# Seven products of half the tokens in place of eight in the MLP's second product

## The chip, the cores and the metric

The kernel runs on one core of a Trainium2 chip. Its engines work side by side: TensorE (PE, with its weight loads PEld) multiplies matrices, VectorE (DVE), ScalarE (ACT) and GpSimd (POOL) do the elementwise work, SyncE (SP) issues most DMAs. The metric is the device time of one execution in microseconds (us). The kernel before takes 2743.2 us, the median of 3 runs from 2741.49 to 2745.22.

## The reference

The reference runs two blocks of a hybrid sequence model on 512 tokens of width 1024 in float32: two layers with gated scans and a convolved feed-forward, and then one layer with four mixers and an MLP. Only the end of that last layer is touched here:

```
hn  = rms(x, norm2_g)
hid = square(relu(hn @ w_mlp1))      # [512, 1024] @ [1024, 4096]
x   = x + hid @ w_mlp2               # [512, 4096] @ [4096, 1024]
```

## The kernel before

Activations lie with features on the 128 partitions and the 512 tokens along the free dimension, so the width of 1024 is KD = 8 tiles and the hidden width of 4096 is 32 tiles. To keep float32 accuracy at the speed of the type fp32r, every operand of a large product is split in two: a high half, rounded by ACT (`activation(..., AF.Copy)`), and a low half, the rest, taken by DVE as a subtraction. A product of a 128 x 128 block of weights with a tile of activations is then three matmuls, high x high, high x low and low x high (`mm3`, which calls `mm`, line 257). They are called split matmuls here, in contrast to the matmuls of small fp32 operands, of which the trace keeps two records each.

`gemm` makes one output tile of 128 features: `weights` loads eight blocks (128 x 1024, 512 KB) through SP into wr, ACT writes wh (line 245), DVE writes wl (line 246), and PE adds up all inner tiles in one of the two banks `pd` of PSUM.

`mlp` works in two halves of 16 hidden tiles. In each, 16 calls of `gemm` make hidden tiles (24 split matmuls each); DVE takes a tile from PSUM times the norm's factor (line 394), squares its positive part (line 1140), and the tile is split into xh (line 286, ACT) and xl (line 287, DVE). Then 8 calls of `gemm` with 48 split matmuls each make the second product of this half, and DVE adds it to the tiles mac, which hold the residual x. After the second half each mac goes to the output. POOL has no part in it.

Pools hand out buffers in turn: wr has 3, wh and wl 2 each, `pd`, `pr` and `pl` 2 banks each. The order in which the instructions stand on each engine is made by the framework's scheduler from the program; each engine then runs its own list strictly in that order, and an instruction that waits holds up all behind it. Three places of that order, before and now, are shown with the change.

Of the kernel before, what the change touches and what calls it, by code (L numbers as in the profile page):

```python
# [8 lines left out]
F32 = mybir.dt.float32  # L9
F32R = mybir.dt.float32r  # L10
U8 = mybir.dt.uint8
AF = mybir.ActivationFunctionType
ALU = mybir.AluOpType
# [4 lines left out]
P = 128  # L18
T = 512
D = 1024  # L20
KD = 8
# [3 lines left out]
LN_NQ = math.log(64.0 ** -0.5)  # L25
DFF1 = 2816
NF1 = 22


def _cols(v):  # L30
# [143 lines left out]
class Net:  # L174
# [77 lines left out]
        self.mm(ps, lo, xh, start=False, stop=stop)  # L252

    def mm(self, *a, **k):
        """a matmul; those of a paced stretch are queued behind the steps of a scan, a few after each"""
        if not self.pace:
            return self.nc.tensor.matmul(*a, **k)  # L257
        with self.tc.issue_after(self.pace[0]):
            self.nc.tensor.matmul(*a, **k)  # L259
        self.paced += 1  # L260
        if self.paced % PACE == 0:
            self.pace.pop(0)

    def gemm(self, srcs, xs, lo="v", m=P):
        bank = self.bank("pd")
        ps = bank[:m]
        nk = sum(s.shape[1] for s in srcs)
        k = 0
        for s in srcs:
            hi, lw = self.weights(s, lo)  # L270
            for i in range(s.shape[1]):
                self.mm3(ps, hi[:, i], lw[:, i], xs[k][0], xs[k][1], k == 0, k == nk - 1)
                k += 1
        return bank

    def split(self, src, gain=None, lo="v", pool=None):
        pl, th, tl = (self.xs, "xs", "xs") if pool is None else (pool[0], f"h{pool[1]}", f"l{pool[1]}")
# [47 lines left out]
        return st["xs"], rb  # L325

    def norm2_end(self, st):
        """the final norm of the first block and the first of the second in one"""
        nc = self.nc
        r, o = self.rtile(), self.rtile()  # L330
        pa, pb = self.sumsq_bc(st["a"]), self.sumsq_bc(st["b"])
        self.rsqrt(r, pa, 1.0 / D, 0)
        nc.vector.tensor_tensor(o, r, r, op=ALU.mult)
        nc.vector.tensor_tensor(o, o, pb, op=ALU.mult)
        self.rsqrt(o, o, 1.0 / D, 0)
        nc.vector.tensor_tensor(o, o, r, op=ALU.mult)
        return st["xs"], o, r
# [57 lines left out]
        return out  # L395

    def gdn_small(self, l, xs, rb, sp):
        """token-major gates of all heads: columns (c, d*4+h)"""
        nc = self.nc
        ps = self.gemm([self.I[f"w_ba{l}"]], xs, m=16)  # L400
        bt = sp.tile([16, T], F32, name=self.nmx("bt"), tag="bt")
# [74 lines left out]

    @staticmethod
    def pair(t, width, b, first, off, n):
        """columns off .. off + n of a tile [P, 2 * width], blocks of b taken in turn from its halves, from half `first` at the start"""
        return bass.AP(tensor=t.tensor, offset=t.offset + off + first * width, ap=[list(t.ap[0]), [2 * b, n // (2 * b)], [b + (1 - 2 * first) * width, 2], [1, b]])  # L480

    def gdn_inverse(self, l, h, sm, gp, front):
# [336 lines left out]
            return self.norm2_end(st) if last else self.norm_end(st)  # L819

    def gemm_tok(self, w, xs, n, rb, pool, tmp, tag):
        """a bank [tokens, 4, n]"""
        t = self.evac(self.gemm([w], xs, m=n)[:n], rb[:n], pool, *tmp, part=n)
        ps = self.bank(tag, shape=(P, 4, n))
        for c in range(4):
            self.nc.tensor.transpose(ps[:, c], t[:, c * P:(c + 1) * P], self.mk("ident")[:n, :n])
        return ps

    def fold_final(self):
        """fin * norm1 gains, used while the last FFN of the first block leaves"""  # L830
        self.fg = self.cp.tile([P, KD], F32, name="fg1")
        self.nc.vector.tensor_tensor(self.fg, self.col("fin", 0, 8), self.col("n1", 0, 8), op=ALU.mult)

# [295 lines left out]
    def mlp(self, state):  # L1129
        nc, tc = self.nc, self.tc  # L1130
        V, A = nc.vector, nc.scalar
        xs, rb = state
        M1, M2 = self.I["w2_m1"], self.I["w2_m2"]
        with tc.tile_pool(name="ml", bufs=1) as ml:
            acc = []
            for half in range(2):
                hs = []
                for m in range(16):
                    h = self.evac(self.gemm([M1[16 * half + m]], xs), rb, ml, "mh", 2)
                    V.scalar_tensor_tensor(h, h, 0.0, h, op0=ALU.max, op1=ALU.mult)  # L1140
                    hs.append(self.split(h, pool=(ml, m)))
                for m in range(KD):
                    ps = self.gemm([M2[m][:, 16 * half + a:16 * half + a + 8] for a in (0, 8)], hs)
                    if half == 0:
                        a = ml.tile([P, T], F32, name=self.nmx("mac"), tag=f"mac{m}")
                        nc.scalar.dma_start(a, self.xd[m])
                        V.tensor_tensor(a, a, ps, op=ALU.add)
                        acc.append(a)
                    else:
                        V.tensor_tensor(acc[m], acc[m], ps, op=ALU.add)  # L1150
                        nc.sync.dma_start(self.O["out"][m], acc[m])


def place_tables(nc):
    """Loads of activation tables, each for the longest run of functions that one set serves"""
    from concourse.hw_specs import get_activation_tables

    sets = {n: {str(f) for f in fs} for n, fs in get_activation_tables("trn2").items()}
# [26 lines left out]
    for i, (b, l) in enumerate(work):  # L1185
        out = []
# [33 lines left out]
```

## Time and profile before

| | |
|---|---|
| profiled execution | span 2742.3 us |
| median of the runs | 2743.2 us, 0.9 us above the span |
| busy in the span | PE 96%, DVE 57%, ACT 41%, POOL 12% |
[...]
| DMA | 254.13 MB, mean 93 GB/s |

The span runs from the first to the last instruction of the one execution that the profiler recorded. The MLP is its end, from about 2399 us on: the hidden tiles of the two halves lie up to about 2487 us and from 2564 to 2651 us, the second products behind them. Lines are numbered as in the kernel printed above. A matmul's duration in the trace reaches from its start until its result is complete; the next one starts earlier, so the time that one costs PE is the distance of two starts. DMA issues and semaphores are not counted as busy.

### The profile page before, as it was taken

How to read it: one execution, taken by the hardware profiler on the slowest of the kernel's cores; microseconds unless marked ns; L12 is line 12 of the kernel's file. 1: busy time of each engine (PE TensorE's matmuls, PEld its weight loads, DVE VectorE, ACT ScalarE, POOL GpSimd, SP SyncE). 2: the span in 40 equal slices, each digit the busy share in tenths (PEclk: the TensorE clock that was granted, in tenths of full speed). 3: DMA queues.
4: the chain of work that ended last, by engine and by line, in shares of the span. 5: the costliest groups of instructions: out<-in, count | busy, mean ns of one | idle time of the engine just before them, and what ended most of it. 6: DMA issues, size and time to landing. Idle time of an engine off the chain costs nothing.

```text
span 2742.3 us, 32455 instructions
## 1 busy us (share of the span) xinstructions
PE 2645.3 (96%) x12674; PEld 2178.6 (79%) x12674; DVE 1556.6 (57%) x2234; ACT 1124.7 (41%) x1511; POOL 329.2 (12%) x282
## 2 busy tenths in 40 slices
PE   7999899999999979998999999999999999999999
PEld 4788788878888857887888788888777788888887
DVE  6778764455554366778644555534874444553442
ACT  6545544343333255455443433333446443332221
POOL 1112320001110011122200011100100111000000
PEclk9999989999999999999999999999999999999999
DMA  4112212253223332111123423234411232433332
GB/s 149 62 49 67 62 39 68 88 167 100 94 98 114 121 89 70 55 61 54 39 76 101 160 95 100 93 121 127 145 64 51 82 96 94 140 129 99 94 104 88
DMA packets 99064, 254.13 MB, mean 93 GB/s; under 512 B 10016, under 2 KB 31520, under 8 KB 98656
## 3 DMA queue, kind: packets, MB, share of 16 engines
q1 hardware_dynamic: 66960, 215.17, 24.5%
q10 hardware_dynamic: 31568, 35.85, 4.5%
q8 instruction: 100, 1.64, 0.2%
q0 software_dynamic: 384, 1.05, 0.1%
q14 instruction: 52, 0.43, 0.1%
HBM read 238.36 MB, written 12.62 MB: 92 GB/s over the span
## 4 chain that ended last, share of the span: by engine, by line
PE 49%; ACT 1%; DVE 0%; issue 0%; POOL 0%; ACTq 0%; DVEq 0%; POOLq 0%
PE pd L257 45%; PE ph L1065 1%; PE pl L1053 1%; PE pd L259 1%; ACT wh L245 0%; PE pr L1061 0%; ACT L1179 0%; PE pl L972 0%; PE ph L682 0%; PE pl L843 0%; DVE wl L246 0%; ACT rb L294 0%; ACT rb L295 0%; PE pl L1015 0%; PE ph L1039 0%
## 5 line engine op out<-in xcount | busy, mean ns | idle before, releaser
L257 PE MATMUL pd<-xh,wh 128*128 128x512 f32 (+1 forms) x3186 | 1265.8, 398 | 36.3 <-DVE raw L449 14.3
L257 PE MATMUL pd<-xh,wl 128*128 128x512 f32 (+1 forms) x3188 | 1258.0, 395 | 2.6 <-DVE wl L246 2.3
L257 PE MATMUL pd<-xl,wh 128*128 128x512 f32 (+1 forms) x3186 | 1253.7, 394 | 2.1 <-DVE xl L290 2.0
L245 ACT ACTIVATE wh<-wr 128x1024 fp32r<-128x1024 f32 (+5 forms) x449 | 434.9, 969 | 1011.3 <-PE pd L257 866.8
L257 PEld LDWEIGHTS pd<-xh,wh 128*128 128x128 f32 (+1 forms) x3186 | 600.2, 188 | 178.8 <-issue 20.9
L257 PEld LDWEIGHTS pd<-xl,wh 128*128 128x128 f32 (+1 forms) x3186 | 600.3, 188 | 139.2 <-issue 7.2
L257 PEld LDWEIGHTS pd<-xh,wl 128*128 128x128 f32 (+1 forms) x3188 | 600.0, 188 | 138.7 <-DVE wl L246 5.0
L246 DVE TENSOR_TENSOR wl<-wr,wh 128x1024 fp32r<-128x1024 f32 (+5 forms) x449 | 521.7, 1162 | 250.3 <-ACT wh L245 244.1
L1179 ACT ACT_TABLE_LOAD x116 | 148.8, 1283 | 8.7 <-issue 4.4
L394 DVE TENSOR_TENSOR g<-pd,rb 128x512 f32<-128x512 f32 x64 | 44.3, 692 | 158.2 <-PE pd L257 148.1
L803 POOL TENSOR_TENSOR fs<-fs,rb 128x512 f32<-128x512 f32 x44 | 56.9, 1294 | 506.3 <-ACT fs L802 506.3
L682 PE MATMUL ph<-pq,kc 128*128 128x128 f32 x448 | 74.8, 313 | 19.6 <-POOL er L569 6.7
L797 DVE TENSOR_TENSOR fg<-pd,rb 128x512 f32<-128x512 f32 x44 | 30.5, 693 | 109.9 <-PE pd L257 107.0
L682 PEld LDWEIGHTS ph<-pq,kc 128*128 128x128 f32 x448 | 66.7, 213 | 26.4 <-issue 19.2
L687 POOL TENSOR_TENSOR pq<-pq,f 128x512 f32<-128x512 f32 x48 | 58.8, 1225 | 230.7 <-PE ph L682 211.5
L805 DVE TENSOR_TENSOR fs<-fs,pd 128x512 f32<-128x512 f32 x44 | 30.3, 688 | 90.0 <-POOL fs L803 90.0
L801 DVE SCALAR_TENSOR_TENSOR fs<-fg,cv,fs 128x512 f32<-128x512 f32 x88 | 65.9, 749 | 3.6 <-ACT fs L799 1.9
L802 ACT ACTIVATE fs<-fs 128x512 f32<-128x512 f32 x44 | 27.8, 632 | 85.5 <-DVE fs L801 85.5
L394 DVE TENSOR_TENSOR mh<-pd,rb 128x512 f32<-128x512 f32 x32 | 22.1, 692 | 70.2 <-PE pd L257 68.8
L680 ACT COPY kc<-qk 128x512 f32<-128x512 f32 x56 | 36.9, 659 | 52.2 <-PE ph L682 44.5
L454 DVE SCALAR_TENSOR_TENSOR qk<-raw,cv,qk 128x512 f32<-128x512 f32 x64 | 54.1, 858 | 2.6 <-ACT qk L452 2.2
L684 DVE COPY_PREDICATED att<-um,ph 128x512 f32<-128x512 uint8 x56 | 41.2, 736 | 21.5 <-PE ph L682 21.2
(332 smaller groups left out, 2442.5 us busy)
## 6 DMA issues: line engine op xcount, KB each, us to landing
wr<-in_w_in_dram SPq DMA_DIRECT2D x126, 512.0 KB, 3.3
wr<-in_w_up_dram SPq DMA_DIRECT2D x88, 512.0 KB, 3.3
wr<-in_w_m_dram SPq DMA_DIRECT2D x64, 512.0 KB, 3.8
wr<-in_w_dn_dram SPq DMA_DIRECT2D x32, 512.0 KB, 3.6
wr<-in_w_gt_dram SPq DMA_DIRECT2D x32, 512.0 KB, 3.3
wr<-in_w_out_dram SPq DMA_DIRECT2D x24, 512.0 KB, 3.4
xd<-xn ACTq DMA_DIRECT2D x40, 256.0 KB, 2.0
xo<-xd ACTq DMA_DIRECT2D x32, 256.0 KB, 2.8
```

What stands on the lines that cost most here:

```text
L245: nc.scalar.activation(hi, raw, AF.Copy)
L246: (nc.vector if lo == "v" else nc.gpsimd).tensor_tensor(lw, raw, hi.bitcast(F32), op=ALU.subtract)
L257: return self.nc.tensor.matmul(*a, **k)
L394: self.nc.vector.tensor_tensor(out, ps, rb, op=ALU.mult)
L454: V.scalar_tensor_tensor(o, raw[:, j:j + T], self.col(f"dnc{l}_{j}", ch), o, op0=ALU.mult, op1=ALU.add)
L680: A.copy(kc.rearrange("p (n e b) -> p n e b", e=2, b=hh), self.pair(qk, T, hh, 0, 0, T))
L682: PE.matmul(pl[:, c], kc[:, c * P:(c + 1) * P], self.pair(pq, T, hh, 1, c * P, P), start=True, stop=True)
L684: V.copy_predicated(att, self.um[:, o:o + P].unsqueeze(1).to_broadcast([P, 4, P]), pl)
L687: (G if hh > 1 else V).tensor_tensor(halves(pq, hh, True), halves(pq, hh, True), tot(F, n, 0, n + 1, hh), op=ALU.mult)
L801: nc.vector.scalar_tensor_tensor(g, gp[:, j:j + T], self.col(f"fc{l}_{j}", m), g, op0=ALU.mult, op1=ALU.add)
L803: nc.gpsimd.tensor_tensor(g, g, rb, op=ALU.mult)
L1179: nc.scalar.preload_act_table_set(s)
```

## The change

The second product is now made in four chunks of eight hidden tiles. In each chunk a pair of hidden tiles (inner index) and a pair of output tiles, with the tokens cut into two halves of TH = 256, form a 2 x 2 problem, and Strassen's scheme makes it from seven products in place of eight. `combos` makes the seven operands of a pair of hidden tiles, split into high and low halves of 256 columns (four sums on DVE, three copies on ACT, three low halves on DVE). `weights7` loads the weights of two output tiles (wr and wq), makes four sums of them on POOL in ws, and the high and low halves of all seven on ACT and DVE. `gemm7` multiplies: each product is 4 inner pairs x 3 matmuls of 256 columns; several products share a bank, and ACT copies three intermediate sums out into s. `add7` adds the four banks (five sums on DVE) and s (two sums on POOL) to mac. `mlp` makes the ninth hidden tile of a chunk, the first of the next one, ahead of the chunk's products.

```diff
+    def combos(self, x0, x1, pool):
+        nc = self.nc
+        V, A = nc.vector, nc.scalar
+        X = pool.tile([P, 7, 2, TH], F32R, name=self.nmx("xc"), tag="xc", bufs=NXC)
+        t = pool.tile([P, 4, TH], F32, name=self.nmx("xt"), tag="xt", bufs=1)
+        b11, b12, b21, b22 = x0[:, :TH], x0[:, TH:], x1[:, :TH], x1[:, TH:]
+        V.tensor_tensor(t[:, 0], b12, b11, op=ALU.subtract)
+        V.tensor_tensor(t[:, 1], b22, t[:, 0], op=ALU.subtract)
+        V.tensor_tensor(t[:, 2], b22, b12, op=ALU.subtract)
+        V.tensor_tensor(t[:, 3], b21, t[:, 1], op=ALU.subtract)
+        for a, n, src in ((4, 1, x0[:, None, :TH]), (5, 2, x1.rearrange("p (a b) -> p a b", a=2)), (0, 4, t)):
+            A.activation(X[:, a:a + n, 0], src, AF.Copy)
+            V.tensor_tensor(X[:, a:a + n, 1], src, X[:, a:a + n, 0].bitcast(F32), op=ALU.subtract)
+        return X
+    def weights7(self, src0, src1, q):
+        nc = self.nc
+        V, A, G = nc.vector, nc.scalar, nc.gpsimd
+        n = src0.shape[1]
+        j = n // 2
+        r0 = self.wp.tile([P, 8, P], F32, name=self.nmx("wr"), tag="wr", bufs=3)[:, :n]
+        r1 = q.tile([P, 8, P], F32, name=self.nmx("wq"), tag="wq", bufs=2)[:, :n]
+        nc.sync.dma_start(r0, src0)
+        nc.sync.dma_start(r1, src1)
+        t0, t1 = (q.tile([P, 2, 4, P], F32, name=self.nmx("ws"), tag=f"ws{i}", bufs=1)[:, :, :j] for i in range(2))
+        a1, a2 = (r.rearrange("p (j e) c -> p e j c", e=2) for r in (r0, r1))
+        G.tensor_tensor(t1[:, 0], a2[:, 0], a2[:, 1], op=ALU.add)
+        G.tensor_tensor(t0[:, 0], a1[:, 0], a2[:, 0], op=ALU.subtract)
+        G.tensor_tensor(t0[:, 1], t1[:, 0], a1[:, 0], op=ALU.subtract)
+        G.tensor_tensor(t1[:, 1], a1[:, 1], t0[:, 1], op=ALU.subtract)
+        w = {}
+        for pl, tag, bufs, src, names in ((self.wp, "", 2, a1, (1, 2)), (q, "s", 3, t0, (7, 6)), (q, "a", 1, a2[:, 1:2], (4,)), (q, "s", 3, t1, (5, 3))):
+            e = len(names)
+            hi, lo = (pl.tile([P, 8, P] if pl is self.wp else [P, e, 4, P], F32R, name=self.nmx(t), tag=t + tag, bufs=bufs) for t in ("wh", "wl"))
+            if pl is self.wp:
+                hi, lo = (t.rearrange("p (e j) c -> p e j c", e=2) for t in (hi, lo))
+            hi, lo = hi[:, :, :j], lo[:, :, :j]
+            A.activation(hi, src, AF.Copy)
+            V.tensor_tensor(lo, src, hi.bitcast(F32), op=ALU.subtract)
+            for i, k in enumerate(names):
+                w[k] = (hi[:, i], lo[:, i])
+        return w
+    def gemm7(self, src0, src1, xc, q, sp):
+        nc = self.nc
+        w = self.weights7(src0, src1, q)
+        half = lambda tag: self.bank(tag, (P, TH))
+        s = sp.tile([P, 3, TH], F32, name=self.nmx("sc"), tag="sc", bufs=NSC)
+        def prod(ps, i, start=True):
+            hi, lo = w[i]
+            k = {1: 4, 2: 5, 3: 6, 4: 3, 5: 0, 6: 1, 7: 2}[i]
+            n = len(xc)
+            for j, x in enumerate(xc):
+                a = {} if start else {"skip_group_check": True}
+                self.mm(ps, hi[:, j], x[:, k, 0], start=start and j == 0, stop=False, **a)
+                self.mm(ps, hi[:, j], x[:, k, 1], start=False, stop=False, **a)
+                self.mm(ps, lo[:, j], x[:, k, 0], start=False, stop=j == n - 1, **a)
+        c, r, b, d = half("pr"), half("pd"), half("pl"), half("pr")
+        prod(c, 2)
+        prod(r, 1)
+        nc.scalar.activation(s[:, 0], r, AF.Copy)
+        prod(b, 7)
+        nc.scalar.activation(s[:, 2], b, AF.Copy)
+        prod(r, 6, False)
+        nc.scalar.activation(s[:, 1], r, AF.Copy)
+        prod(b, 4, False)
+        prod(r, 5, False)
+        prod(d, 3)
+        return c, r, b, d, s
+    def add7(self, a0, a1, parts):
+        V, G = self.nc.vector, self.nc.gpsimd
+        c, r, b, d, s = parts
+        lo, up = slice(0, TH), slice(TH, T)
+        for a, h, ps in ((a0, lo, c), (a1, lo, b), (a0, up, r), (a1, up, r), (a0, up, d)):
+            V.tensor_tensor(a[:, h], a[:, h], ps, op=ALU.add)
+        G.tensor_tensor(a0[:, lo], a0[:, lo], s[:, 0], op=ALU.add)
+        G.tensor_tensor(a1, a1, s[:, 1:3].rearrange("p a b -> p (a b)"), op=ALU.add)
...
-            acc = []
-            for half in range(2):
-                hs = []
-                for m in range(16):
-                    h = self.evac(self.gemm([M1[16 * half + m]], xs), rb, ml, "mh", 2)
-                    V.scalar_tensor_tensor(h, h, 0.0, h, op0=ALU.max, op1=ALU.mult)
-                    hs.append(self.split(h, pool=(ml, m)))
-                for m in range(KD):
-                    ps = self.gemm([M2[m][:, 16 * half + a:16 * half + a + 8] for a in (0, 8)], hs)
-                    if half == 0:
-                        a = ml.tile([P, T], F32, name=self.nmx("mac"), tag=f"mac{m}")
-                        nc.scalar.dma_start(a, self.xd[m])
-                        V.tensor_tensor(a, a, ps, op=ALU.add)
-                        acc.append(a)
-                    else:
-                        V.tensor_tensor(acc[m], acc[m], ps, op=ALU.add)
-                        nc.sync.dma_start(self.O["out"][m], acc[m])
+            acc, hid, xc = [], {}, []
+            for m in range(KD):
+                a = ml.tile([P, T], F32, name=self.nmx("mac"), tag=f"mac{m}")
+                nc.scalar.dma_start(a, self.xd[m])
+                acc.append(a)
+
+            def up(m):
+                h = self.evac(self.gemm([M1[m]], xs), rb, ml, "mh", 4)
+                V.scalar_tensor_tensor(h, h, 0.0, h, op0=ALU.max, op1=ALU.mult)
+                hid[m] = h
+
+            for m in range(32):
+                if m not in hid:
+                    up(m)
+                if m % 2:
+                    xc.append(self.combos(hid[m - 1], hid[m], ml))
+                if m % 8 == 7:
+                    if m < 31:
+                        up(m + 1)
+                    for i in range(0, KD, 2):
+                        self.add7(acc[i], acc[i + 1], self.gemm7(M2[i][:, m - 7:m + 1], M2[i + 1][:, m - 7:m + 1], xc, ml, ml))
+                    xc = []
+            for m in range(KD):
+                nc.sync.dma_start(self.O["out"][m], acc[m])
```

The scheduler orders anew all that follows the last output projection. Names below carry the program's numbers. The first place is the end of POOL's list, behind the last mixer's sums (acc). Before:

```order
L1105 TENSOR_TENSOR acc_14068<-acc_14068,g_17170 128x512
L1105 TENSOR_TENSOR acc_14069<-acc_14069,g_17219 128x512
L1105 TENSOR_TENSOR acc_14070<-acc_14070,g_17268 128x512
L1105 TENSOR_TENSOR acc_14071<-acc_14071,g_17317 128x512
L1215 UNCONDITIONAL_BRANCH
```

Now there are 96 operations more. For the first chunk (wr and wq the loaded weights of a pair of output tiles, ws their sums, sc the copied intermediate sums):

```order
L307 TENSOR_TENSOR ws_18116<-wq_18112 128x512
L308 TENSOR_TENSOR ws_18115<-wr_18111,wq_18112 128x512
L309 TENSOR_TENSOR ws_18115<-ws_18116,wr_18111 128x512
L310 TENSOR_TENSOR ws_18116<-wr_18111,ws_18115 128x512
L308 TENSOR_TENSOR ws_18240<-wr_18236,wq_18237 128x512
L307 TENSOR_TENSOR ws_18241<-wq_18237 128x512
L309 TENSOR_TENSOR ws_18240<-ws_18241,wr_18236 128x512
L310 TENSOR_TENSOR ws_18241<-wr_18236,ws_18240 128x512
L308 TENSOR_TENSOR ws_18365<-wr_18361,wq_18362 128x512
L361 TENSOR_TENSOR mac_17741<-mac_17741,sc_18137 128x256
L307 TENSOR_TENSOR ws_18366<-wq_18362 128x512
```

Eight operations for two pairs' weights come first; from then on each pair's four are mixed with the two sums into mac of the pair before.

The second place is DVE's list among the hidden tiles, mh being a hidden tile and wl low halves of weights. Before, for three tiles:

```order
L394 TENSOR_TENSOR mh_18266<-pd_18235,rb_17729 128x512
L1140 SCALAR_TENSOR_TENSOR mh_18266<-mh_18266 128x512
L246 TENSOR_TENSOR wl_18314<-wr_18312,wh_18313 128x1024
L287 TENSOR_TENSOR xl_18270<-mh_18266,xh_18269 128x512
L394 TENSOR_TENSOR mh_18304<-pd_18273,rb_17729 128x512
L1140 SCALAR_TENSOR_TENSOR mh_18304<-mh_18304 128x512
L246 TENSOR_TENSOR wl_18352<-wr_18350,wh_18351 128x1024
L287 TENSOR_TENSOR xl_18308<-mh_18304,xh_18307 128x512
L394 TENSOR_TENSOR mh_18342<-pd_18311,rb_17729 128x512
L1140 SCALAR_TENSOR_TENSOR mh_18342<-mh_18342 128x512
L246 TENSOR_TENSOR wl_18382<-wr_18380,wh_18381 128x1024
```

Now, behind the first read of the sixth tile (mh_17982) of the first chunk, xt and xc being sums and operands of a pair of hidden tiles:

```order
L1231 SCALAR_TENSOR_TENSOR mh_17982<-mh_17982 128x512
L249 TENSOR_TENSOR wl_18034<-wr_18032,wh_18033 128x1024
L287 TENSOR_TENSOR xt_17986<-mh_17982,xt_17986 128x256
L288 TENSOR_TENSOR xt_17986<-mh_17982,mh_17948 128x256
L292 TENSOR_TENSOR xc_17985<-mh_17982,xc_17985 128x2x256
L289 TENSOR_TENSOR xt_17986<-mh_17982,xt_17986 128x256
L319 TENSOR_TENSOR wl_18126<-ws_18115,wh_18125 128x1024
L482 TENSOR_TENSOR mh_18028<-pd_17997,rb_17729 128x512
L292 TENSOR_TENSOR xc_17985<-xt_17986,xc_17985 128x4x256
L319 TENSOR_TENSOR wl_18134<-ws_18116,wh_18133 128x1024
L1231 SCALAR_TENSOR_TENSOR mh_18028<-mh_18028 128x512
L249 TENSOR_TENSOR wl_18080<-wr_18078,wh_18079 128x1024
```

The two low halves of sums of weights (wl_18126 and wl_18134, from ws) stand ahead of wl_18080, the low half of the ninth tile's own weights.

The third place is PE's list where hidden tiles end and products begin. Before, pd_18311 is the last hidden tile of the half and pd_18349 the first output tile:

```order
L257 MATMUL pd_18311<-xh_17722,wh_18313 128x512
L257 MATMUL pd_18311<-xl_17723,wh_18313 128x512
L257 MATMUL pd_18311<-xh_17722,wl_18314 128x512
L257 MATMUL pd_18349<-xh_17775,wh_18351 128x512
L257 MATMUL pd_18349<-xl_17776,wh_18351 128x512
L257 MATMUL pd_18349<-xh_17775,wl_18352 128x512
```

Now, pd_18031 is the eighth hidden tile, pl_18140 the first pair's product 7 and pd_18077 the ninth hidden tile, which needs wl_18080:

```order
L260 MATMUL pd_18031<-xh_17722,wl_18034 128x512
L260 MATMUL pl_18140<-xc_17825,wh_18125 128x256 x2
L260 MATMUL pl_18140<-xc_17825,wl_18126 128x256
L260 MATMUL pl_18140<-xc_17905,wh_18125 128x256 x2
L260 MATMUL pl_18140<-xc_17905,wl_18126 128x256
L260 MATMUL pd_18077<-xh_17416,wh_18079 128x512
L260 MATMUL pd_18077<-xl_17417,wh_18079 128x512
L260 MATMUL pl_18140<-xc_17985,wh_18125 128x256 x2
L260 MATMUL pl_18140<-xc_17985,wl_18126 128x256
L260 MATMUL pd_18077<-xh_17416,wl_18080 128x512
```

Matmuls of the first product now stand between those of the second: nine short ones before the third of the ninth tile.

## Rows read from the trace of the kernel before

**Rows 1.** first section of the page: busy us (share) x instructions of each engine.
```profile
PE 2645.3 (96%) x12674; PEld 2178.6 (79%) x12674; DVE 1556.6 (57%) x2234; ACT 1124.7 (41%) x1511; POOL 329.2 (12%) x282
```

**Rows 2.** windows, second products: PE, PEld, DVE, ACT, POOL busy, clock, DMA.
```profile
2487.50:2564.20 76.70, 76.70 (x340) 63.53 (x339) 21.98 (x21) 15.04 (x15) 0.00 (x0) 1.00 0.33 98
2651.50:2738.30 86.80, 86.79 (x383) 71.52 (x382) 24.89 (x25) 16.17 (x16) 0.00 (x0) 1.00 0.30 94
```

**Rows 3.** chain that ended last, its last row: start, us, engine, line.
```profile
2400.72 337.59 PE pd L257 x1488
```

**Rows 4.** groups by form, the MLP, loads of weights: busy us, mean ns.
```profile
L257 PEld LDWEIGHTS pd<-xh,wl 128*128 128x128 f32 x498 | 93.5, 188 | 19.3
```

**Rows 5.** timeline, fp32 matmuls: start us, us, engine, line, operands.
```profile
175.56 0.39 PE L715 MATMUL ph<-pq,hs 128*128 128x128 f32 x2
175.78 0.39 PE L711 MATMUL ph<-att,it 128*128 128x128 f32 x2
...
2027.68 1.03 PE L1039 MATMUL ph<-vcmp,npct 128*128 128x256 f32 x4
```

**Rows 6.** line 1039: duration ns min/median/max, first and last start.
```profile
L1039 PE MATMUL ph<-vcmp,npct x8: 379/379/483, 2021.5 to 2028.3; 128*128 128x256 f32 x8
```

**Rows 7.** groups by form, the MLP, DVE.
```profile
L246 DVE TENSOR_TENSOR wl<-wr,wh 128x1024 fp32r<-128x1024 f32 x61 | 74.5, 1222 | 63.9 <-ACT wh L245 63.9
L1140 DVE SCALAR_TENSOR_TENSOR mh<-mh 128x512 f32<-128x512 f32 x32 | 22.2, 692 | 1.1
L394 DVE TENSOR_TENSOR mh<-pd,rb 128x512 f32<-128x512 f32 x32 | 22.1, 692 | 70.2 <-PE pd L257 68.8 <-ACT rb L295 1.4
L287 DVE TENSOR_TENSOR xl<-mh,xh 128x512 fp32r<-128x512 f32 x32 | 21.8, 684 | 0.0
```

**Rows 8.** groups by form from 2190 us on, ACT.
```profile
L245 ACT ACTIVATE wh<-wr 128x1024 fp32r<-128x1024 f32 x92 | 97.6, 1061 | 330.4 <-PE pd L257 264.0 <-issue 66.4
L286 ACT ACTIVATE xh<-mh 128x512 fp32r<-128x512 f32 x32 | 20.3, 634 | 17.7 <-DVE mh L1140 17.7
L245 ACT ACTIVATE wh<-wr 128x256 fp32r<-128x256 f32 x22 | 8.8, 402 | 0.0
```

**Rows 9.** groups by form, whole span, POOL.
```profile
L803 POOL TENSOR_TENSOR fs<-fs,rb 128x512 f32<-128x512 f32 x44 | 56.9, 1294 | 506.3 <-ACT fs L802 506.3
L1073 POOL TENSOR_TENSOR nyo<-nyo,nt 128x256 f32<-128x256 f32 x8 | 5.9, 732 | 74.9 <-DVE nt L1071 74.6
```

**Rows 10.** timeline near 466 us, POOL and DVE.
```profile
466.59 1.29 POOL L769 TENSOR_TENSOR g<-g,g 128x512 f32<-128x512 f32 x1 [11.01 <-DVE g L768]
466.68 2.27 DVE L246 TENSOR_TENSOR wl<-wr,wh 128x1024 fp32r<-128x1024 f32 x1 [0.17 <-ACT wh L245]
```

**Rows 11.** timeline near 2190 us, POOL and DVE.
```profile
2190.10 0.68 DVE L1104 TENSOR_TENSOR g<-g,pd 128x512 f32<-128x512 f32 x1
2190.69 0.42 DVE L246 TENSOR_TENSOR wl<-wr,wh 128x256 fp32r<-128x256 f32 x1
2190.85 2.84 POOL L1105 TENSOR_TENSOR acc<-acc,g 128x512 f32<-128x512 f32 x2 [7.17 <-DVE g L1104]
2191.03 0.68 DVE L1104 TENSOR_TENSOR g<-g,pd 128x512 f32<-128x512 f32 x1
2191.63 0.92 DVE L246 TENSOR_TENSOR wl<-wr,wh 128x256 fp32r<-128x256 f32 x1
```

**Rows 12.** timeline of the end: PE, DVE, the queue of SP.
```profile
2737.90 0.39 PE L257 MATMUL pd<-xh,wl 128*128 128x512 f32 x1
2738.33 0.69 DVE L1150 TENSOR_TENSOR mac<-mac,pd 128x512 f32<-128x512 f32 x1 [8.79 <-PE pd L257]
2739.04 0.33 SPq L1151 DMA_DIRECT2D out_dram<-mac  x1
```

**Rows 13.** issues of DMA: count, KB each, us to landing.
```profile
wr<-in_w_m_dram SPq DMA_DIRECT2D x64, 512.0 KB, 3.8
```

**Rows 14.** window with gaps on PE; columns as in rows 2.
```profile
2174.00:2192.00 18.00, 15.29 (x83) 10.93 (x82) 10.19 (x15) 10.96 (x14) 5.41 (x4) 1.00 0.29 87
```

More of the change, by code (lines that the diff above doesn't have):

```diff
@@ L27 @@
 NF1 = 22
+TH = T // 2
+NXC = 4
+NSC = 1
 def _cols(v):
```

## Prediction

> **What bounds the kernel now.** I read the busy shares first: PE works in 96% of the span [rows 1]. The windows of the MLP come next: in the two windows of its second product PE is busy without a gap, POOL does nothing, and DVE and ACT are busy for under a third [rows 2]. The chain that ended last closes with one unbroken run of 1488 matmuls in 337.59 us, so one matmul costs 226.9 ns there [rows 3]. [...] The last view is the timeline of places where DVE and POOL meet [rows 10, 11], because the change brings POOL into a part where it was idle.
>
> **What is removed and added on PE.** The second product has 768 matmuls of 512 columns: 768 x 0.2269 = 174.3 us. Each call of gemm7 has 7 products x 4 inner pairs x 3 = 84 matmuls of 256 columns, and 16 calls make 1344. The trace has no split matmul of 256 columns. The nearest rows are fp32 matmuls, which the trace records twice each: one record of 256 columns lasts 379 ns [rows 6], nearly the 0.39 us of a split matmul of 512 [rows 12], so a record of N fp32 columns streams about as long as 2N split ones. Two bounds follow. Four records of 256 columns take 1.03 us, so (1.03 - 0.38) / 3 = 217 ns each [rows 5]; half is 108 ns. If the 10 ns by which a split matmul exceeds that belong to each matmul, not to its columns, it is 108 + 10 = 118 ns. Halving 226.9 gives 113.4 ns, which I take. The loads of weights keep that pace: one lasts 188 ns [rows 4], yet pairs of 128-column records, each with its own load, start 0.22 us apart [rows 5], 0.11 each. So 1344 x 0.1134 = 152.4 us, 21.9 us less; with the bounds 29.2 less (108 ns) or 15.7 less (118 ns).
>
> [...]
>
> **What is added beside PE.** From the rows of DVE, ACT and POOL [rows 7 to 9], with 0.42 us for DVE and 0.40 for ACT at 256 columns [rows 11, 8]: a call of gemm7 costs DVE three low halves of 1.22, one of 0.68 and five sums of 0.42 = 6.4; ACT three high halves of 1.06, one of 0.63 and three copies of 0.40 = 5.0; POOL five operations of 1.29 and one of 0.73 = 7.2. The pair's combinations cost DVE 4 x 0.42 + 0.42 + 0.68 + 1.22 = 4.0 in place of two splits, 1.4. In a chunk of eight hidden tiles PE needs 8 x 24 x 0.2269 + 336 x 0.1134 = 81.7 us; DVE 8 x (0.69 + 0.69 + 1.22) + 16.0 + 25.8 = 62.6; ACT about 37; POOL 28.8. Each alone fits under PE. The weights come in the same 64 loads of 512 KB, each landing in 3.8 us [rows 13], so DMA costs nothing. The loads of mac and the stores of the result only move.
>
> DVE and POOL do not fit side by side. A low half of 1.22 lasts 2.27 when a POOL operation began 0.09 before it [rows 10]: 0.09 + 2.27 - 1.22 = 1.14, so POOL held DVE off for some 1.15 us. Where DVE has one operand in PSUM it runs beside POOL unharmed (0.68), while the next one with both in SBUF takes 0.92 instead of 0.42 [rows 11]. Of DVE's 62.6 us a chunk, 5.5 + 8.4 read PSUM; the other 48.7 exclude POOL, which holds about 4 x (5 x 1.15 + 0.6) = 25.4. Together 74.1 of 81.7 us. But DVE works in order and stands still while it waits: if none of its PSUM work falls beside POOL, it needs 62.6 + 25.4 = 88.0, 6.3 more than PE.
>
> [...]
>
> **Where PE waits.** Every chunk passes from hidden tiles to products. Count from the end of its sixth tile. By the order of the changed kernel DVE then has 13 operations up to wl_18080, the low weights of the ninth tile (five of 1.22, five of about 0.69, three of 0.42): 10.8 us, less twelve overlaps of 0.09 (a free operation starts before the last one ends, [rows 11]), 9.9 with the drain. PE wants it after two tiles, six to nine short matmuls and two long ones: 12.4. But five operations of POOL stand in that stretch, 5 x 1.15 less 0.7 beside a read of PSUM = 5.1: 2.6 us late. The next nine of DVE, 5.4 us, with three of POOL, 2.8, end 8.2 later, when PE has had 22 long and some 17 short matmuls, 6.9: 1.3 late. So 3.9 if POOL wins each meeting, 0 if DVE does, and up to 8 if the loads or ACT come late as well. POOL's four operations for one pair follow one another, so one is nearly always pending: I take 3.5.
>
> In the rest of the products DVE has 25.6 us, 7.9 of it on PSUM, and POOL holds 15.6, against 291 x 0.1134 + 5.4 = 38.4 of PE: 33.3 to 41.2. Behind a held DVE stand its sums, and those free the banks that PE's products of the pair after next wait for; behind POOL's sum of one pair stands ACT's copy of the next (one sc buffer), and behind that copy the high halves. Stepping through it with the durations above, PE loses about 1.7 and 1.1 at two such banks: I take 3.0 a chunk (0 to 6).
>
> The last chunk has no ninth tile as cover: PE has 5.4 less, DVE 2.6 less, so 2.8 more waiting, and before the last pair's product 6 the chain of two sums, POOL and the copy (0.2 + 0.84 + 1.29 + 0.40 = 2.7) stands against ten matmuls, 1.1. Together 4.5 (2 to 7). The tail grows from one sum of 0.69 [rows 12] to two of 0.42 and POOL's 1.29: 1.4. PE's waits are short and the clock should stay: it was 1.00 over 18 us in which PE was busy for 15.29 [rows 14].
>
> Sum: -21.9 + 4 x 3.5 + 4 x 3.0 + 4.5 + 1.4 = +10.0. The profiled execution took 2742.3 us of span; the median of the runs, 2743.2, is 0.9 above it. So 2742.3 + 0.9 + 10.0 = 2753 us.
>
> **Rivals.**
> [...]
> Second, DVE and POOL become the bound of the whole chunk. None of the PSUM work falls beside POOL, and DVE also idles 2 x 1.7 us in the first two pairs of tiles, where it waits for PE (9.2 of 10.9 us a pair) and POOL has nothing to do: 88.0 + 3.4 = 91.4 a chunk, 9.7 over PE. Then -21.9 + 38.8 + 5.9 = +23, 2766 us; this mechanism decides against the change from 4.0 us a chunk on. Late loads or copies on top give 2776.
> Third, loads of weights are not hidden and each matmul lasts the 188 ns of its load: 1344 x 0.188 = 252.7, +78, 2821 us. Against it stand the 0.11 of rows 5.
> Fourth, gain and waits cancel, at 4.0 us a chunk: 2743.
>
> **Chances.** The forecast 0.41 (its own range 2748 to 2762), the first rival 0.27, the fourth 0.16, the second 0.13, the third 0.03. A measurement of this kernel tells 0.2%, 5.5 us, from no change: faster is the first rival, 0.27; the same the fourth, 0.16; slower the rest, 0.57. All best ends together are -29.2 + 2 + 1.4 = -26, all worst -15.7 + 32 + 24 + 7 + 1.4 = +49. Both at once are unlikely; 2731 to 2776 leaves out the far part of the first rival and the third.
>
> **What would show it.** Right: matmuls of 256 columns start about 113 ns apart; PE has gaps in the MLP where the releaser is DVE, first before wl of the ninth tile of each chunk and then before products that wait for a bank; low halves of 1.22 us have a mean well above that, and POOL's operations too. Wrong: a spacing of 118 or more, or gaps that end with ACT or a DMA, or no gaps and an MLP shorter by 15 us. [...]

## The result, and the profile after

The changed kernel takes 2762.0 us (median of 4 runs, 2760.4 to 2765.8) against 2743.9 for the kernel before (now the median of 4 runs): 18.1 us slower, ratio 1.0074 with a 95% interval from 1.0060 to 1.0088. The forecast was 2753, the range 2731 to 2776. The profiled execution has a span of 2761.5 us. Its first section, which answers to [rows 1]:

```profile
PE 2643.9 (96%) x13250; PEld 2202.0 (80%) x13250; DVE 1684.9 (61%) x2410; ACT 1176.9 (43%) x1607; POOL 478.8 (17%) x378
```

POOL works 150 us more and DVE 128 us more; PE has 576 matmuls more. What the shorter matmuls cost stands in the chain of waits (start, us, engine, line, count), which answers to [rows 3]:

```profile
2461.46 1.44 PE pr L260 x12
```

Twelve matmuls of 256 columns take 1.44 us, 120 ns each. So 1344 of them are 161.3 us, against 174.3 for the 768 of before: PE's work falls by 13.0 us.

The rest is waiting. The list of PE's waits in the MLP (who waits, for what: us in total, times, longest):

```profile
PE pd L260 <- DVE wl L249: 10.0, 4, 3.5
PE pd L260 <- DVE mac L360: 5.8, 8, 1.3
PE pd L260 <- ACT sc L344: 1.5, 1, 1.5
```

These are the three largest of six rows, which come to 18.9 us. Ten of them end with the low weights of a hidden tile (L249), as forecast. The list does not show what comes behind such a wait. PE's timeline at the first passage from hidden tiles to products (start, us, operation; the bracket is the idle time and what ended it):

```profile
2433.45 0.39 PE L260 MATMUL pl<-xc,wh 128*128 128x256 f32 x2
2433.68 0.28 PE L260 MATMUL pl<-xc,wl 128*128 128x256 f32 x1
2437.41 0.80 PE L260 MATMUL pd<-xh,wl 128*128 128x512 f32 x1 [3.45 <-DVE wl L249]
2438.00 0.63 PE L260 MATMUL pd<-xh,wh 128*128 128x512 f32 x1
2438.42 0.63 PE L260 MATMUL pd<-xl,wh 128*128 128x512 f32 x1
...
```

PE waits 3.45 us for the ninth tile's low weights. Behind that, starts are 0.43 us apart and not 0.227: the granted clock is 0.50 from 2437.41 to 2440.20 us, here called half clock. The windows (columns as in [rows 2]; the third number from the end is the granted clock as a share of full speed) say the same of three passages, against a stretch of products in the last row:

```profile
2433.90:2440.40 6.50, 3.05 (x8) 2.43 (x8) 6.50 (x5) 2.42 (x3) 5.85 (x4) 0.74 0.25 74
2524.90:2532.50 7.60, 4.55 (x14) 3.53 (x13) 7.60 (x7) 2.42 (x3) 5.14 (x3) 0.78 0.25 69
2615.60:2624.80 9.20, 6.15 (x17) 4.73 (x16) 9.20 (x9) 3.05 (x4) 5.14 (x3) 0.63 0.24 64
2441.00:2520.00 79.00, 77.65 (x495) 70.50 (x494) 59.63 (x79) 29.86 (x42) 29.80 (x20) 1.00 0.31 97
```

Who made DVE late stands on the timeline of ACT, DVE and POOL at that place, which answers to [rows 10]:

```profile
2428.18 1.07 ACT L318 ACTIVATE wh<-ws 128x1024 fp32r<-128x1024 f32 x1 [4.50 <-POOL ws L309]
...
2429.27 1.32 DVE L319 TENSOR_TENSOR wl<-ws,wh 128x1024 fp32r<-128x1024 f32 x1 [3.52 <-ACT wh L318]
...
2432.32 2.28 POOL L308 TENSOR_TENSOR ws<-wr,wq 128x512 f32<-128x512 f32 x1 [2.80 <-DVE xc L292]
...
2433.39 1.76 DVE L1231 SCALAR_TENSOR_TENSOR mh<-mh 128x512 f32<-128x512 f32 x1
...
2434.56 1.71 POOL L307 TENSOR_TENSOR ws<-wq 128x512 f32<-128x512 f32 x1
2435.07 2.28 DVE L249 TENSOR_TENSOR wl<-wr,wh 128x1024 fp32r<-128x1024 f32 x1
...
2436.35 2.13 POOL L309 TENSOR_TENSOR ws<-ws,wr 128x512 f32<-128x512 f32 x1
2437.28 1.49 DVE L286 TENSOR_TENSOR xt<-mh 128x256 f32<-128x256 f32 x1
```

The square of a hidden tile (L1231) lasts 1.76 us and not 0.69, the low half 2.28 and not 1.22, a sum of 256 columns 1.49 and not 0.42, each beside a POOL sum for the second pair of output tiles, which PE needs only later. POOL's sums last 1.7 to 2.3 us and not 1.29. So each of the two holds the other off. Two of the expectations below call this the port; what the traces show of it are these times. Up to the end of the ninth tile's low half (2437.35 us) DVE is held for 2.2 us by this. That is not all at this first passage: before it DVE stood idle for 3.52 us, since the next operation of its list (L319) waited for the end of a chain: POOL began when the weights had landed (2425.29 us) and made two sums, then ACT made their high half (L318). At the second and the third passage DVE does not stand idle; there five operations are held, 5.4 us together. Three of them, at the second:

```profile
2515.14 1.50 DVE L287 TENSOR_TENSOR xt<-mh,xt 128x256 f32<-128x256 f32 x1
...
2522.91 2.31 DVE L319 TENSOR_TENSOR wl<-ws,wh 128x1024 fp32r<-128x1024 f32 x1
...
2525.75 2.29 DVE L249 TENSOR_TENSOR wl<-wr,wh 128x1024 fp32r<-128x1024 f32 x1
```

Over the whole MLP the low halves of [rows 7] have become longer by form:

```profile
L249 DVE TENSOR_TENSOR wl<-wr,wh 128x1024 fp32r<-128x1024 f32 x29 | 41.9, 1444 | 4.0 <-ACT wh L248 4.0
L319 DVE TENSOR_TENSOR wl<-ws,wh 128x1024 fp32r<-128x1024 f32 x32 | 41.6, 1302 | 24.5 <-ACT wh L318 24.5
...
L319 DVE TENSOR_TENSOR wl<-wr,wh 128x1024 fp32r<-128x1024 f32 x16 | 23.3, 1458 | 0.0
```

and at the end POOL's sum stands between the last sum of DVE and the store, which answers to [rows 12]:

```profile
2756.51 1.26 POOL L362 TENSOR_TENSOR mac<-mac,sc 128x512 f32<-128x512 f32 x1 [4.73 <-DVE mac L360]
2756.76 1.37 SPq L1246 DMA_DIRECT2D out_dram<-mac  x2
```

From the starts of all matmuls of the MLP, each distance less 0.2269 or 0.120 us, PE lost 32.7 us (0.4 in the kernel before): 16.1 at the first three passages (10.0 of waiting, 6 of half clock), 5.7 in the products of the first three chunks, 9.3 in the last chunk, 1.6 at the start. With -13.0 of work and 1.8 of tail the MLP is 21.2 us longer: what PE waits is paid in full. What lies ahead of it was 2.0 us shorter in this execution (the sum for the MLP's norm starts at 2394.5 us, before at 2396.5), hence 19.2 in the span.

### The profile page after: what moved, and what is told of

Its sections match the earlier page's. It is cut to its first block, busy times and chain, and to the rows that moved or that the text cites. A ratio compares the mean times of both kernels' runs of the same rounds, so it can differ in the third digit from the quotient of the medians.

```text
span 2761.5 us, 34063 instructions
## 1 busy us (share of the span) xinstructions
PE 2643.9 (96%) x13250; PEld 2202.0 (80%) x13250; DVE 1684.9 (61%) x2410; ACT 1176.9 (43%) x1607; POOL 478.8 (17%) x378
## 4 chain that ended last, share of the span: by engine, by line
PE 44%; DVE 4%; ACT 1%; issue 1%; DMA 0%; POOL 0%; POOLq 0%; ACTq 0%; SPq 0%; DVEq 0%
PE pd L260 38%; DVE wl L319 1%; PE pl L260 1%; PE pr L260 1%; DVE wl L249 1%; PE ph L1153 1%; PE pd L262 1%; PE pl L1141 1%; DVE mac L360 0%; ACT wh L248 0%; DVE xc L292 0%; PE pr L1149 0%; ACT wh L318 0%; DVE mh L1231 0%; ACT L1274 0%
## 5 line engine op out<-in xcount | busy, mean ns | idle before, releaser
L260 PE MATMUL pd<-xh,wh 128*128 128x512 f32 (+2 forms) x2930 | 1168.5, 399 | 37.1 <-DVE raw L537 14.9
L260 PE MATMUL pd<-xh,wl 128*128 128x512 f32 (+2 forms) x2932 | 1161.3, 396 | 12.6 <-DVE wl L249 12.3
L260 PE MATMUL pd<-xl,wh 128*128 128x512 f32 (+2 forms) x2930 | 1156.4, 395 | 2.3 <-DVE xl L378 2.3
L248 ACT ACTIVATE wh<-wr 128x1024 fp32r<-128x1024 f32 (+4 forms) x417 | 400.9, 962 | 815.9 <-PE pd L260 671.5
L260 PEld LDWEIGHTS pd<-xh,wh 128*128 128x128 f32 (+2 forms) x2930 | 553.5, 189 | 169.6 <-issue 20.3
L260 PEld LDWEIGHTS pd<-xh,wl 128*128 128x128 f32 (+2 forms) x2932 | 553.5, 189 | 140.7 <-DVE wl L249 16.6
L260 PEld LDWEIGHTS pd<-xl,wh 128*128 128x128 f32 (+2 forms) x2930 | 553.7, 189 | 128.5 <-issue 7.2
L249 DVE TENSOR_TENSOR wl<-wr,wh 128x1024 fp32r<-128x1024 f32 (+4 forms) x417 | 489.4, 1174 | 193.1 <-ACT wh L248 186.8
L885 DVE TENSOR_TENSOR fg<-pd,rb 128x512 f32<-128x512 f32 x44 | 30.5, 693 | 109.8 <-PE pd L260 107.0
L260 PE MATMUL pd<-xc,wh 128*128 128x256 f32 x384 | 73.9, 286 | 7.3 <-DVE mac L360 5.8
L260 PEld LDWEIGHTS pd<-xc,wh 128*128 128x128 f32 x384 | 61.0, 192 | 9.6 <-DVE mac L360 7.4
L318 ACT ACTIVATE wh<-ws 128x1024 fp32r<-128x1024 f32 x32 | 33.9, 1058 | 56.9 <-POOL ws L309 40.8
```

Source lines behind the costliest of these rows:

```text
L248: nc.scalar.activation(hi, raw, AF.Copy)
L249: (nc.vector if lo == "v" else nc.gpsimd).tensor_tensor(lw, raw, hi.bitcast(F32), op=ALU.subtract)
L318: A.activation(hi, src, AF.Copy)
L885: nc.vector.tensor_tensor(gp[:, 1:T + 1], ps, rb, op=ALU.mult)
```

## The experiments

Each kernel was timed beside the kernel before on its chip (medians 2742 to 2743 us; 2746, a single run, beside the kernel with quarters).

**The price of a short matmul.** The kernel before, its second product in halves:

```diff
...
+                for h in range(2):
+                    c = slice(h * TH, h * TH + TH)
+                    self.mm3(ps[h], hi[:, i], lw[:, i], xs[k][0][:, c], xs[k][1][:, c], k == 0, k == nk - 1)
...
```

> The kernel before, with each split matmul of 512 columns of its second product cut into two of 256 (768 become 1536, each half of the tokens in a bank of its own, same weights). No Strassen, no work on POOL. Theory: a split matmul costs a fixed 13 ns on top of its columns (226.9 ns for 512, 120 ns for 256 as in the changed kernel), whatever kernel it stands in. Then 1536 x 0.120 = 184.3 us in place of 174.3: +10.0 us, 2753 to 2754 us, spacing 120 ns. Rival: the 120 ns belong to the changed kernel (its operands in xc, its changes of bank); then 113.4 ns here, and the time stays at 2743 to 2745 us.

Measured: 2756.4 us, ratio 1.0054 (1.0036 to 1.0073), by the interval 10 to 20 us more; the profiled execution took 2753.1, as forecast, the median is 2.4 us above the forecast's upper end. In the chain three take 0.36 us:

```profile
2477.64 0.36 PE pd L258 x3
```

That is 120 ns again. PE's matmuls of the second product sum to 184.2 us, 9.9 more than before, without a wait. The 120 ns belong to the matmul, not to Strassen's operands.

**Below 256 columns.** The same in four quarters of 128 columns:

```diff
-                for h in range(2):
-                    c = slice(h * TH, h * TH + TH)
+                for h in range(4):
+                    c = slice(h * P, h * P + P)
...
```

> The kernel before with each split matmul of its second product cut into four of 128 columns (768 become 3072, each quarter of the tokens in a bank of its own, one of which has a single buffer, so PE may also wait up to 0.8 us at each of the 16 output tiles). Theory: the spacing is 13.1 ns + 0.4167 ns a column at any width, as 226.9 at 512 and 120 at 256 give: 66.4 ns, 204 us in place of 174.3, 2773 to 2790 us. Rival: below 256 columns the loads of weights set the pace; fp32 records of 64 and of 128 columns, each with its own load, are both 111 ns apart in the trace; then 3072 x 0.111 = 341 us, 2910 us or more.

Measured: 2909.1 us in one run, matmuls 111.6 ns apart (mean of 3070 distances). In the chain, and where the stream begins:

```profile
2475.28 0.34 PE pr L258 x3
```

```profile
2473.49 0.22 PE L258 MATMUL pd<-xh,wh 128*128 128x128 f32 x1
...
2473.55 0.28 PE L258 MATMUL pd<-xl,wh 128*128 128x128 f32 x1
...
2473.66 0.27 PE L258 MATMUL pr<-xh,wh 128*128 128x128 f32 x1
```

My theory of a fixed 13 ns at any width (226.9 and 120 give 13.1 ns and 0.418 ns a column) fell; the rival holds. At 128 columns the loads set the pace: the second matmul of the stream starts 58 ns behind the first, so the columns take no longer than that, but from the second on each starts 54 to 61 ns behind the start of its own load, and the loads start 108 to 111 ns apart. That is nearly the 111.6 ns from one matmul to the next. From 512 to 256 columns the distance nearly halves (226.9 to 120), from 256 to 128 it hardly falls.

**POOL taken out.** The changed kernel without the six POOL sums of a call (results incomplete by these sums; ACT copies stand in for the weights' sums):

```diff
-        G.tensor_tensor(t1[:, 0], a2[:, 0], a2[:, 1], op=ALU.add)
...
+        A.activation(t0, a1, AF.Copy)
+        A.activation(t1, a2, AF.Copy)
...
-        G.tensor_tensor(a0[:, lo], a0[:, lo], s[:, 0], op=ALU.add)
-        G.tensor_tensor(a1, a1, s[:, 1:3].rearrange("p a b -> p (a b)"), op=ALU.add)
```

> The changed kernel without any work on POOL in the MLP: the four sums of weights of a pair of output tiles are left out (ACT copies the loaded weights into ws instead, two operations of 1.06 us, so that the chain from load to high half stays), and so are the two sums of s into mac. DVE and PE have the same work as in the changed kernel. Theory: PE's waits of 3.6, 3.2 and 3.2 us for the ninth tile's low weights come from DVE being held off by POOL, and the stretches at half clock behind them follow from the waits. Then DVE's low halves of 128 x 1024 are back at 1.22 us, the three waits are under 0.5 us, the 16.4 us lost at the three passages nearly all return, some 5 of the 8.4 us of the last chunk too, and 1.3 us of the tail: 2738 to 2742 us. Rival: the waits come from DVE's order alone (13 operations ahead of wl_18080); then they stay at 2.5 us or more and the time at 2756 us or above.

Measured: 2732.8 us, ratio 0.9962 (0.9948 to 0.9977), below the expected range, since the waits at the banks went too. PE lost 2.1 us in the whole MLP, and the clock is 1.00 in it. In this kernel eleven of DVE's operations from the sixth tile's first read on stand ahead of the low half of the ninth tile's weights and not twelve (the square of the seventh tile, 0.69 us, stands behind it), and PE uses it 1.4 us after it is done at the first passage and 2.6 us at the other two. So DVE's work and its order alone cost nothing there. The run takes away two things at once, POOL's work beside DVE and DVE's wait for what POOL makes; the next one brings back the first alone.

**POOL put back, read by nobody.** The same kernel with four POOL sums a call into a tile that is never read. PE, DVE and ACT have the same lists, operation by operation:

```diff
+        u = q.tile([P, 4, P], F32, name=self.nmx("wu"), tag="wu", bufs=1)
+        G.tensor_tensor(u, a2[:, 0], a2[:, 1], op=ALU.add)
+        G.tensor_tensor(u, a1[:, 0], a2[:, 0], op=ALU.subtract)
+        G.tensor_tensor(u, u, a1[:, 0], op=ALU.subtract)
+        G.tensor_tensor(u, a1[:, 1], u, op=ALU.subtract)
```

> The kernel without work on POOL (2733 us; sums of weights and of s left out, ACT's copies in their place) with four sums of weights per call put back on POOL, into a tile that nobody reads. The lists of PE, DVE and ACT are the same, operation by operation; nothing that is computed waits for POOL, but wr and wq come free only when POOL has read them. Theory of the port: DVE is held off again for 4 x 1.15 us a call, the low halves of 1.22 us get longer, and PE waits at the passages, with stretches at half clock: 2748 to 2760 us. Rival: POOL cost time by the chain from load to sum to high half, not by the port; then the time stays at 2733 us (within 4).

Measured: 2767.2 us, ratio 1.0092 (1.0077 to 1.0107): 34 us more than without, above the expected range. PE lost 37.3 us in the MLP against 2.1. The same four DVE operations, first in the kernel without POOL and then in this one:

```profile
2429.48 0.69 DVE L292 TENSOR_TENSOR xc<-mh,xc 128x512 fp32r<-128x512 f32 x1 [1.65 <-ACT xc L291]
2430.09 0.42 DVE L289 TENSOR_TENSOR xt<-mh,xt 128x256 f32<-128x256 f32 x1
2430.43 2.36 DVE L317 TENSOR_TENSOR wl<-ws,wh 128x1024 fp32r<-128x1024 f32 x2
```

```profile
2428.11 1.30 POOL L310 TENSOR_TENSOR wu<-wu,wr 128x512 f32<-128x512 f32 x1
...
2428.24 1.72 DVE L292 TENSOR_TENSOR xc<-mh,xc 128x512 fp32r<-128x512 f32 x1 [1.41 <-ACT xc L291]
...
2429.49 1.62 POOL L311 TENSOR_TENSOR wu<-wr,wu 128x512 f32<-128x512 f32 x1
...
2429.88 1.51 DVE L289 TENSOR_TENSOR xt<-mh,xt 128x256 f32<-128x256 f32 x1
...
2431.19 1.37 POOL L308 TENSOR_TENSOR wu<-wq 128x512 f32<-128x512 f32 x1
2431.32 3.46 DVE L322 TENSOR_TENSOR wl<-ws,wh 128x1024 fp32r<-128x1024 f32 x2
```

And the first sections of the pages of the two, in the same order:

```profile
PE 2636.3 (96%) x13250; PEld 2199.1 (80%) x13250; DVE 1635.8 (60%) x2410; ACT 1205.5 (44%) x1639; POOL 329.1 (12%) x282
```

```profile
PE 2652.0 (96%) x13250; PEld 2207.1 (80%) x13250; DVE 1685.8 (61%) x2410; ACT 1206.8 (44%) x1639; POOL 438.5 (16%) x346
```

DVE has 2410 operations in both and is busy 50.0 us longer: 0.78 us for each of the 64 sums that it does not depend on. POOL's 64 sums take 109.4 us, 27 more than at 1.29 each, so the exclusion falls on both engines. No other comparison here changes POOL's presence alone; it shows the exclusion by itself. What the chain of load, POOL's sums and ACT's high half costs at the first passage of the changed kernel no run shows by itself. wr and wq come free later as well, but ACT's copies of wr wait 11.0 us for loads in this kernel and 11.8 in the one without POOL: the loads are not what came late.

**The sums on DVE.** All six sums of a call go from POOL to DVE; the result is complete:

```diff
-        V, A, G = nc.vector, nc.scalar, nc.gpsimd
+        V, A, G = nc.vector, nc.scalar, nc.vector
...
-        V, G = self.nc.vector, self.nc.gpsimd
+        V, G = self.nc.vector, self.nc.vector
```

> The changed kernel with the six sums of a call of gemm7 on DVE in place of POOL; the result is complete. DVE then has 4 x 0.69 + 0.42 + 0.69 = 3.9 us more a call, 78 us a chunk against 83.9 of PE, but nothing holds it off. Theory of the port: a sum costs DVE 0.69 us instead of a hold of 1.15, so the passages get better though DVE has more work: waits of 1 to 2 us in place of 3.3, 2750 to 2758 us. Rival (DVE's load decides, not the port): more waits everywhere, 2764 us or more.

Measured: 2736.1 us over 8 runs, ratio 0.9978 (0.9968 to 0.9989): faster than the kernel before, and 14 us below the expected range; the rival, DVE's load, is refuted. PE's waits in the MLP:

```profile
PE pd L260 <- ACT sc L344: 1.3, 2, 1.1
PE pd L260 <- DVE mac L360: 0.7, 3, 0.2
```

Its first section says why DVE can bear it:

```profile
PE 2632.4 (96%) x13250; PEld 2195.4 (80%) x13250; DVE 1686.3 (62%) x2506; ACT 1175.7 (43%) x1607; POOL 328.5 (12%) x282
```

DVE is busy for 1686.3 us, with 96 operations more than in the changed kernel, which had 1684.9. POOL's help saved DVE nothing: the time for which it held DVE off was as long as the sums themselves. What differs is the place, and that DVE does not wait for POOL's sums at the first passage. POOL makes its sums as soon as weights land, in a row; in DVE's list they stand apart, between other work, and the three passages lose nothing (PE lost 5.7 us in all).

**Which sums.** Two kernels with one half of that edit each. Only the weights' sums on DVE (weights7):

```diff
-        V, A, G = nc.vector, nc.scalar, nc.gpsimd
+        V, A, G = nc.vector, nc.scalar, nc.vector
```

> The changed kernel with the four sums of weights of a call on DVE, and the two sums of s into mac left on POOL; the result is complete. With all six on DVE the three passages lost nothing and the time was 2736 us. Theory: what costs is the sums of weights on POOL, since they stand in the passages, where DVE has no slack; the mac sums come behind the products, where it has. DVE has 78.1 - 4 x 1.1 = 73.7 us a chunk and is held for 4 x 1.7 = 6.9 by the mac sums: no wait at a passage, 2734 to 2739 us, like all six on DVE. Rival: any hold counts, since DVE is at 78 of 84 us; then 2742 us or more.

Measured: 2738.9 us, ratio 0.9989 (0.9979 to 0.9998), as the theory has it; its interval overlaps that of all six on DVE. Only the sums into mac on DVE (add7):

```diff
-        V, G = self.nc.vector, self.nc.gpsimd
+        V, G = self.nc.vector, self.nc.vector
```

> The counterpart: the two sums into mac on DVE, the four sums of weights left on POOL; the result is complete. Theory: the passages wait as in the changed kernel (3.2 to 3.6 us, then half clock), the waits of 0.8 us at the banks shrink: 2755 to 2762 us. Rival: the mac sums and the copy that stands behind them were the cause; then 2745 us or less.

Measured: 2760.0 us, ratio 1.0064 (1.0047 to 1.0080), as in the changed kernel. The weights' sums on POOL are the cause: by the timelines they hold DVE off and, at the first passage, come late as well.

**More cover at the passage.** Two hidden tiles made ahead of the products, POOL as in the changed kernel:

```diff
-                h = self.evac(self.gemm([M1[m]], xs), rb, ml, "mh", 4)
+                h = self.evac(self.gemm([M1[m]], xs), rb, ml, "mh", 5)
...
                     if m < 31:
                         up(m + 1)
+                        up(m + 2)
```

> The changed kernel with two hidden tiles of the next chunk made ahead of the products in place of one (mh gets a fifth buffer); POOL keeps its sums. Theory: at the passage PE has 5.4 us more to do while DVE has 2.6 us more, so the waits of 3.2 to 3.6 us shrink below 1 us, and with them the stretches at half clock go: 10.0 + 6.3 = 16.3 us back at the three passages, the last chunk as before: 2745 to 2750 us. Rival: the wait only moves, to the tenth tile or to the first products, and the clock falls there: 2756 us or above.

Measured: 2756.7 us, ratio 1.0049 (1.0034 to 1.0064). The rival was right that the wait only moves. PE waits now, in the two largest rows, for the operands and weights of the first products, in pieces of 0.8 and 0.9 us:

```profile
PE pr L260 <- DVE wl L319: 3.1, 4, 0.8
PE pl L260 <- DVE xc L292: 3.0, 4, 0.9
```

The rival had the clock wrong: it is 1.00 there. PE lost 23.0 us in the MLP in place of 32.7; against the changed kernel's ratio the intervals just overlap. Cover helps little while POOL still holds DVE.

**The clock by itself.** The kernel before, with the low half of some hidden tiles' weights taken again, so that PE waits for it:

```diff
+        for _ in range(1 + self.late):
             (nc.vector if lo == "v" else nc.gpsimd).tensor_tensor(lw, raw, hi.bitcast(F32), op=ALU.subtract)
...
+                    self.late = {3: 4, 6: 5, 9: 6, 12: 8}.get(m, 0)
```

> The kernel before, in which DVE takes the low half of the weights of four hidden tiles of each half 4, 5, 6 and 8 times more than needed (1.13 us each, the same values again), so that PE has to wait for them for different times, some 0 to 6 us; no Strassen, no work on POOL. Theory: a wait of over 3 us is itself what the half clock follows from: behind it 512-column matmuls start 0.427 us apart for some 8 to 13 matmuls (1.6 to 2.6 us lost), behind waits of about 1 us none do. Rival: the half clock comes from something else in the changed kernel (its mix of short matmuls and DVE, ACT and POOL all at work); then matmuls are 0.227 apart right behind every wait here.

Measured, in one execution (2786.8 us): three waits of 2.00, 4.10 and 4.12 us are followed by 6, 11 and 12 starts 0.427 us apart, some twenty waits of 0.3 to 1.4 us by none. Around the first long one:

```profile
2408.06 0.40 PE L260 MATMUL pd<-xl,wh 128*128 128x512 f32 x1
2410.45 0.79 PE L260 MATMUL pd<-xh,wl 128*128 128x512 f32 x1 [2.00 <-DVE wl L248]
2411.05 0.63 PE L260 MATMUL pd<-xh,wh 128*128 128x512 f32 x1
2411.47 0.63 PE L260 MATMUL pd<-xl,wh 128*128 128x512 f32 x1
...
2413.60 0.40 PE L260 MATMUL pd<-xh,wh 128*128 128x512 f32 x1
2413.83 0.39 PE L260 MATMUL pd<-xl,wh 128*128 128x512 f32 x1
```

and around one of 0.88 us:

```profile
2421.77 0.39 PE L260 MATMUL pd<-xh,wl 128*128 128x512 f32 x1
2423.03 0.47 PE L260 MATMUL pd<-xh,wh 128*128 128x512 f32 x1 [0.88 <-ACT wh L246]
2423.34 0.39 PE L260 MATMUL pd<-xl,wh 128*128 128x512 f32 x1
```

The mean granted clock is 0.68 from 2408.20 to 2413.50 us, around the wait of 2.00, 0.66 from 2475.40 to 2485.30 us, around that of 4.10, and 1.00 from 2421.90 to 2427.00 us, behind that of 0.88. So half clock follows such a wait without Strassen and without POOL. That only waits of 2 us and more bring it is not so: in the kernel with unread sums it also came behind groups of waits of which none reached 1.5 us (1.37, 0.47 and 1.48 us; 1.27 and 0.71; 1.22 and 0.76).

## Why the prediction was right in sign and short in size

- **PE's work.** Forecast -21.9 us (bounds -29.2 and -15.7), measured -13.0. This is the step that failed: I halved 226.9 ns to 113.4, against 120 measured. The forecast named the other branch (a part that belongs to each matmul, 118 ns) and did not take it, and even that was too low. The fp32 records of [rows 5] did not carry over. If the columns alone take half of the 427 and 213 ns between starts at half clock, an estimate, a split matmul has some 13 ns on top at either width (226.9 - 213.5 and 120 - 106.5), and halving the width does not halve that; a record of 256 fp32 columns, 217 ns, counted as 512 split ones, has 3.5. 1344 x 6.6 ns = 8.9 us, while the whole miss is 8.1 (18.1 against 10.0). That the two agree is luck: losses and tail were 2.2 us too small as well, what lies ahead of the MLP was 2.0 shorter, and the span grew 1.1 more than the median.
- **Exclusion of DVE and POOL.** Right, and now shown (50.0 us of DVE for 64 unread sums, with the same order on PE, DVE and ACT). Low halves have a mean of 1.30 to 1.46 us and return to 1.22 without POOL. The price of 1.15 us a sum was an upper one: DVE pays 0.78 in the mean, and POOL's own sums become 0.42 longer; the forecast let POOL win nearly every meeting.
- **Passages.** Forecast 3.5 us a chunk, at wl of the ninth tile; the waits there cost 3.6, 3.2 and 3.2 us of start distance. But each passage lost some 5 to 6. At the second and the third the mechanism is the one forecast, with five operations held for 5.4 us (forecast 5.1). At the first it is not: 2.2 us of holding and 3.5 of idling for the load, POOL's sums and their high half, which the forecast had only as a possible extra ("if the loads or ACT come late"). That the wait there is of the same size is luck.
- **Clock.** "The clock should stay" failed. [Rows 14] held several short gaps; the change brings single ones of 3.05 to 3.45 us, and 6 us were lost at half clock, a granted 0.50, behind them.
- **Rest of the products.** Forecast 3.0 a chunk, measured 1.8 to 2.1, at two banks (0.86 and 0.77 us, where the stepping had 1.7 and 1.1).
- **Last chunk.** Forecast 3.5 + 3.0 + 4.5 = 11.0, measured 9.3. **Tail:** 1.4 and 1.8.

All losses of PE in the MLP were forecast at 30.5 us and measured at 32.3 beyond before: right as a sum by luck, since a clock term that was missing and banks that were dearer in the forecast cancel. The first rival (0.27, 2729 us: the collisions of DVE and POOL cost PE nothing) is refuted as a mechanism, for 64 POOL sums that nobody reads cost 34 us, yet the kernels without the weights' sums on POOL come near its time (2733 to 2739). The third (loads set the pace at 188 ns) was wrong in size, but the loads do set it at 128 columns, at 111.6.

## What to carry to other kernels

A scheme that trades fewer multiplications for shorter matmuls must be priced with the distance measured at that width: seven eighths of the columns were 93% of the time here, and one halving more would gain next to nothing a matmul (111.6 ns after 120). Work given to POOL was not free for DVE here: operations with both operands in SBUF lasted longer beside it (2.28 us in place of 1.22), 96 POOL sums cost DVE as much as doing them itself, and at worse places; moving them to DVE turned 18 us of loss into 7 us of gain. A long wait of PE was dearer here than its length: each one measured of 2 us and more (2.00 to 4.12) was followed by half clock, and some groups of shorter ones too.

## What was not expected of the hardware

- Split matmuls start 226.9, 120 and 111.6 ns apart at 512, 256 and 128 columns; at a granted clock of 0.50 those of 512 and 256 are 427 and 213 ns apart, 1.88 and 1.78 times as far.
- In the kernel with low halves taken again, a PE wait of 2.00 us was followed by 2.6 us of starts 0.427 us apart, one of 4.10 by 4.7, waits up to 1.4 us by none. In the changed kernel's last chunk two waits of 0.71 and 0.56 us were followed by starts 0.213 us apart, in the kernel with two tiles ahead nearly the same two were not. In the kernel with unread sums, waits of 1.37, 0.47 and 1.48 us were followed by half clock, waits of 0.60, 0.48 and 1.49 were not; what decides between these stays open.
